# Eight experts, two layers: x in two loads of four experts, finer last pieces of w2, stores moved between queues

## Chip, cores and metric

One Trainium2 chip, one core. The metric is device time in microseconds; the time of a kernel is the median of its runs. Engines are named as in the profile: PE (matmul), PEld (weight load of PE), DVE (VectorE), ACT (ScalarE), POOL (GpSimd), SP (SyncE).

## The reference

```python
n_experts, capacity, hidden, expert_hidden = 8, 256, 512, 2048
h = np.matmul(x, w1)        # (8,256,512) @ (8,512,2048)
h = np.maximum(h, 0)
return np.matmul(h, w2).astype(np.float32)   # (8,256,2048) @ (8,2048,512)
```

All inputs and the output are float32. Each expert has 4.19 MB of w1, 4.19 MB of w2, 0.52 MB of x and 0.52 MB of output.

## The kernel before

The kernel works in bf16 on PE. Weights are cast on the way in: `load_w1` (L55) and `load_w2` (L59) issue DMAs from POOL that read f32 and write bf16. One load is 128 rows of 32 KB in memory, one for each partition; w2 of the last expert comes in four pieces of 6, 5, 3 and 2 row groups (a row group is 128 rows of w2, one for each partition). The tag "w1" and the tag "w2" have four buffers each, so a load of expert e waits until expert e - 4 has been used. POOL issues its DMAs in program order: it stands still at the first that has to wait.

x comes in f32 from SP, one load of 512 KB for each expert with rows of 4 KB (`load_x`, L51), four experts ahead. `transpose_x` (L65) casts it on ACT (L67), transposes it on PE in eight 128x128 blocks into one PSUM bank (L71) and copies it out on DVE (L75).

`first_layer` (L77) makes the hidden layer in eight groups of 8 matmuls (L83), each 128x128 weights by 256 columns of x; the relus alternate between ACT (L93) and DVE (L91). `second_layer` (L98) makes 32 matmuls of 512 columns (L107), 16 row groups of w2 times two halves of the rows; DVE copies out one half (L115), ACT the other (L116), and SP stores the expert (L121), or SP and ACT half of it each for the last expert (L118, L119).

The order is written out by hand (`manual_schedule`, L49; L124 to L145): first and second layer of experts 0 to 4 in turn, then the three first layers of experts 5, 6 and 7, then their three second layers. All weight loads are put on POOL ahead of the computation in this same order. The transposes of expert e + 1 stand behind the first layer of expert e on PE. On SP, the load of x of expert e + 4 stands behind the store of expert e. In the text below, w1(3) is w1 of expert 3, and so on.

Of the kernel before, what the change touches and what calls it, by code (L numbers as in the profile page):

```python
# [1 line left out]

# [5 lines left out]


@with_exitstack  # L10
def kernel(
    ctx: ExitStack,
    tc: tile.TileContext,
    x: bass.AP,
    w1: bass.AP,
    w2: bass.AP,
    out: bass.AP,
):
    nc = tc.nc
    P = 128  # L20
    bf = mybir.dt.bfloat16
    f32 = mybir.dt.float32

    E, C, H = x.shape
    F = w1.shape[2]
    MT = C // P
    KT1 = H // P
    KT2 = F // P
    AHEAD = 4


    x_r = x.rearrange("e (p mt) k -> e p mt k", p=P)
    w1_r = w1.rearrange("e (p kt) n -> e p kt n", p=P)
    w2_r = w2.rearrange("e (p kt) n -> e p kt n", p=P)
    out_r = out.rearrange("e (p mt) n -> e p mt n", p=P)

    const = ctx.enter_context(tc.tile_pool(name="const", bufs=1))
    wpool = ctx.enter_context(tc.tile_pool(name="weights", bufs=4))
    xpool = ctx.enter_context(tc.tile_pool(name="xs", bufs=AHEAD))
    tpool = ctx.enter_context(tc.tile_pool(name="xts", bufs=2))  # L40
    hpool = ctx.enter_context(tc.tile_pool(name="hidden", bufs=4))
    opool = ctx.enter_context(tc.tile_pool(name="outs", bufs=3))
    ps_h = ctx.enter_context(tc.tile_pool(name="ps_h", bufs=4, space=bass.MemoryType.PSUM))
    ps_o = ctx.enter_context(tc.tile_pool(name="ps_o", bufs=4, space=bass.MemoryType.PSUM))

    x_sb, w1_sb, w2_sb, xt, ht = {}, {}, {}, {}, {}


    ctx.enter_context(tc.manual_schedule())  # L49

    def load_x(e):  # L51
        x_sb[e] = xpool.tile([P, MT, H], f32, tag="x", name="x_sb")
        nc.sync.dma_start(x_sb[e][:], x_r[e])

    def load_w1(e):  # L55
        w1_sb[e] = wpool.tile([P, KT1, F], bf, tag="w1", name="w1_sb")
        nc.gpsimd.dma_start(w1_sb[e][:], w1_r[e])  # L57

    def load_w2(e):  # L59
        w2_sb[e] = wpool.tile([P, KT2, H], bf, tag="w2", name="w2_sb")  # L60
        cuts = (0, KT2) if e < E - 1 else (0, 6, 11, 14, 16)
        for lo, hi in zip(cuts, cuts[1:]):
            nc.gpsimd.dma_start(w2_sb[e][:, lo:hi, :], w2_r[e, :, lo:hi, :])  # L63

    def transpose_x(e):  # L65
        x_bf = tpool.tile([P, MT, H], bf, tag="xb", name="x_bf")
        nc.scalar.copy(x_bf[:], x_sb[e][:])  # L67
        pt = ps_o.tile([P, KT1, MT, P], bf, tag="ps_o", name="pt_tr")
        for kt in range(KT1):
            for mt in range(MT):  # L70
                nc.tensor.transpose(  # L71
                    pt[:, kt, mt, :], x_bf[:, mt, kt::KT1], identity[:]
                )
        xt[e] = tpool.tile([P, KT1, C], bf, tag="xt", name="xt_sb")
        nc.vector.tensor_copy(xt[e][:], pt[:].rearrange("p k m q -> p k (m q)"))  # L75

    def first_layer(e):  # L77
        ht[e] = hpool.tile([P, KT2, C], bf, tag="ht", name="ht_sb")
        for g in range(KT2 // 2):
            ph = ps_h.tile([P, 2, C], f32, tag="ps_h", name="pt_h")  # L80
            for i in range(2):
                for kt in range(KT1):
                    nc.tensor.matmul(  # L83
                        ph[:, i, :],
                        w1_sb[e][:, kt, 2 * g + i::KT2],
                        xt[e][:, kt, :],
                        start=(kt == 0),
                        stop=(kt == KT1 - 1),
                    )
            if g % 2:  # L90
                nc.vector.tensor_relu(ht[e][:, 2 * g:2 * g + 2, :], ph[:])  # L91
            else:
                nc.scalar.activation(  # L93
                    ht[e][:, 2 * g:2 * g + 2, :], ph[:],
                    mybir.ActivationFunctionType.Relu,
                )

    def second_layer(e):  # L98
        last = e == E - 1
        po = [  # L100
            ps_o.tile([P, H], f32, tag="ps_o", name=f"pt_o{mt}") for mt in range(MT)
        ]
        order = [(kt, mt) for kt in range(KT2) for mt in range(MT)]
        if last:
            order = order[:-4] + [(kt, mt) for mt in range(MT) for kt in (KT2 - 2, KT2 - 1)]
        for kt, mt in order:
            nc.tensor.matmul(  # L107
                po[mt][:],
                ht[e][:, kt, mt * P:(mt + 1) * P],
                w2_sb[e][:, kt, :],  # L110
                start=(kt == 0),
                stop=(kt == KT2 - 1),
            )
        o = opool.tile([P, MT, H], f32, tag="o", name="out_sb")
        nc.vector.tensor_copy(o[:, 0, :], po[0][:])  # L115
        nc.scalar.copy(o[:, 1, :], po[1][:])  # L116
        if last:
            nc.sync.dma_start(out_r[e, :, 0, :], o[:, 0, :])  # L118
            nc.scalar.dma_start(out_r[e, :, 1, :], o[:, 1, :])  # L119
        else:  # L120
            nc.sync.dma_start(out_r[e], o[:])  # L121


    order = []  # L124
    for e in range(E - 3):
        order += [(1, e), (2, e)]
    order += [(1, e) for e in range(E - 3, E)] + [(2, e) for e in range(E - 3, E)]

    for e in range(AHEAD):
        load_x(e)  # L130
    for layer, e in order:
        (load_w1 if layer == 1 else load_w2)(e)
        if (layer, e) == (1, 0):
            identity = const.tile([P, P], bf, name="identity")
            make_identity(nc, identity)
    transpose_x(0)
    for layer, e in order:
        if layer == 1:
            first_layer(e)
            if e + 1 < E:  # L140
                transpose_x(e + 1)
        else:
            second_layer(e)
            if e + AHEAD < E:
                load_x(e + AHEAD)  # L145


# [1 line left out]
_INS = ['x', 'w1', 'w2']  # L149
_OUTS = [((8, 256, 512), 'float32')]  # L150


# [23 lines left out]
```

## Time and profile before

| | |
|---|---|
| median of 11 runs | 186.9 us (186.77 to 188.67) |
| profiled execution | 188.32 us |
| its span, first to last instruction | 186.5 us |
| mean granted PE clock | 0.927 |
| PE busy | 132.9 us (71%) |
| PE weight loads busy | 91.3 us (49%) |
| DVE, ACT, POOL busy | 33.2, 32.6, 10.9 us |
| DMA | 5192 packets, 42.06 MB at the destination |

The span leaves out what lies around the first and last instruction; the profiled execution's own time is 1.8 us longer. In the profile, a timeline line gives start, length, engine, line of the code, operation, output and inputs, count, and in brackets how long the engine had been idle and what ended it. A stretch gives each engine's busy time in a window with the granted clock, the mean busy share of the 16 DMA engines and what they moved. Packet records can overlap, so a DMA share can pass 1. "q0" holds the DMAs that POOL issues, "q1" those of SP, "q10" those of ACT.

### The profile page before, as it was taken

The numbers are of one execution on the slowest core, as the hardware profiler recorded it, in microseconds if no ns is written. First come the engines' busy times: TensorE is split into PE (matmuls) and PEld (weight loads), VectorE is DVE, ScalarE is ACT, GpSimd is POOL, SyncE is SP. The second block draws the span as 40 slices with busy tenths as digits, with TensorE's granted clock in tenths as the row PEclk, the third lists the DMA queues.
The fourth block names the chain that finished last, engine by engine and source line by source line (L and its number), as shares of the span: only waits on it lengthen the run. The fifth ranks groups of instructions, "written<-read, shape, count | busy, mean of one in ns | idle before, by whom it ended". The sixth has DMA issues, their size and how long they took to land.

```text
span 186.5 us, 1894 instructions
## 1 busy us (share of the span) xinstructions
PE 132.9 (71%) x832; PEld 91.3 (49%) x832; DVE 33.2 (18%) x48; ACT 32.6 (18%) x49; POOL 10.9 (6%) x25
## 2 busy tenths in 40 slices
PE   0204959488595988749894795929969695949990
PEld 0103944187232873238741693407969693414440
DVE  0100240113101141101311032011224241010101
ACT  3100330124001240102401123011242421010101
POOL 7300010101000010000201101001000000000000
PEclk9999999999879699966999799995899999988999
DMA  6989999999999999999989899999999999999913
GB/s 222 270 211 249 243 214 225 221 237 240 217 275 212 258 230 220 259 213 264 239 205 281 203 259 235 213 275 211 242 240 225 225 218 197 204 216 263 217 58 114
DMA packets 5192, 42.06 MB, mean 225 GB/s; under 512 B 576, under 2 KB 576, under 8 KB 3264
## 3 DMA queue, kind: packets, MB, share of 16 engines
q0 software_dynamic: 2736, 33.56, 84.6%
q1 hardware_dynamic: 2304, 8.13, 11.6%
q10 hardware_dynamic: 144, 0.26, 0.4%
q8 instruction: 6, 0.10, 0.2%
q14 instruction: 2, 0.02, 0.0%
HBM read 71.30 MB, written 4.19 MB: 405 GB/s over the span
## 4 chain that ended last, share of the span: by engine, by line
PE 55%; DMA 24%; another core or an unknown queue 10%; ACT 3%; issue 2%; POOL 1%; DVE 1%; ACTq 0%; POOLq 0%
PE pt_o L107 28%; PE pt_h L83 26%; DMA w_sb<-in_w_dram 24%; ACT x_bf L67 3%; PE pt_tr L71 2%; DVE xt_sb L75 1%; POOL w_sb L57 1%; DVE out_sb L115 0%; POOL w_sb L63 0%; POOL identity masks.py:199 0%; POOL identity masks.py:197 0%; ACT ht_sb L93 0%; ACTq L116 0%; POOLq masks.py:199 0%
## 5 line engine op out<-in xcount | busy, mean ns | idle before, releaser
L83 PE MATMUL pt_h<-xt_sb,w_sb 128*128 128x256 bf16 x512 | 67.9, 302 | 28.6 <-DMA w_sb<-in_w_dram 27.0
L83 PEld LDWEIGHTS <-w_sb 128*128 128x128 bf16 x512 | 61.8, 149 | 35.9 <-DMA w_sb<-in_w_dram 30.0
L107 PE MATMUL pt_o<-w_sb,ht_sb 128*128 128x512 bf16 x256 | 59.7, 394 | 9.9 <-DMA w_sb<-in_w_dram 9.9
L107 PEld LDWEIGHTS <-ht_sb 128*128 128x128 bf16 x256 | 25.7, 101 | 42.1 <-issue 15.4
L91 DVE TENSOR_SCALAR ht_sb<-pt_h 128x512 bf16<-128x512 f32 x32 | 22.1, 692 | 75.3 <-PE pt_h L83 75.3
L93 ACT ACTIVATE ht_sb<-pt_h 128x512 bf16<-128x512 f32 x32 | 19.1, 597 | 74.8 <-PE pt_h L83 74.8
L116 ACT COPY out_sb<-pt_o 128x512 f32<-128x512 f32 x8 | 4.7, 585 | 72.2 <-PE pt_o L107 72.2
L115 DVE COPY out_sb<-pt_o 128x512 f32<-128x512 f32 x8 | 5.5, 691 | 62.9 <-PE pt_o L107 62.9
L71 PE MATMUL pt_tr<-identity,x_bf 128*128 128x128 bf16 x64 | 5.5, 234 | 10.4 <-ACT x_bf L67 10.4
L71 PEld LDWEIGHTS <-x_bf 128*128 128x128 bf16 x64 | 4.1, 119 | 12.1 <-ACT x_bf L67 12.1
L57 POOL DMA_DIRECT2D w_sb<-in_w_dram x8 | 4.4, 556 | 75.6 <-PE pt_h L83 74.8
L67 ACT CAST x_bf<-x_sb 128x1024 bf16<-128x1024 f32 x8 | 8.3, 1037 | 2.1 <-DMA x_sb<-in_x_dram 2.1
L63 POOL DMA_DIRECT2D w_sb<-in_w_dram x11 | 6.0, 543 | 39.9 <-DMA w_sb<-in_w_dram 24.1
L75 DVE COPY xt_sb<-pt_tr 128x1024 bf16<-128x1024 bf16 x8 | 5.5, 692 | 11.1 <-PE pt_tr L71 11.1
L67 ACT ACT_TABLE_LOAD x1 | 1.3, 1283 | 0.7 <-PEq L160 0.7
masks.py:199 POOL TENSOR_SCALAR_AFFINE_SELECT identity<-identity 128x128 bf16<-128x128 bf16 x1 | 0.3, 287 | 0.1
masks.py:197 POOL MEMSET identity<- 128x128 bf16 x1 | 0.2, 223 | 0.0
L160 POOL MEMSET const-float32-0.0<- 128x1 f32 x1 | 0.1, 98 | 0.2 <-issue 0.2
L160 POOL MEMSET const-bfloat16-1.0<- 128x1 bf16 x1 | 0.1, 101 | 0.0
L160 POOL MEMSET const-uint8-127<- 128x1 uint8 x1 | 0.1, 101 | 0.0
L160 POOL MEMSET const-float32-1.0<- 128x1 f32 x1 | 0.1, 98 | 0.0
## 6 DMA issues: line engine op xcount, KB each, us to landing
w_sb<-in_w_dram POOLq DMA_DIRECT2D x15, 2048.0 KB, 66.3
x_sb<-in_x_dram SPq DMA_DIRECT2D x8, 512.0 KB, 25.6
out_dram<-out_sb SPq DMA_DIRECT2D x7, 512.0 KB, 15.4
w_sb<-in_w_dram POOLq DMA_DIRECT2D x1, 768.0 KB, 70.1
w_sb<-in_w_dram POOLq DMA_DIRECT2D x1, 640.0 KB, 70.1
w_sb<-in_w_dram POOLq DMA_DIRECT2D x1, 384.0 KB, 60.5
w_sb<-in_w_dram POOLq DMA_DIRECT2D x1, 256.0 KB, 51.2
out_dram<-out_sb ACTq DMA_DIRECT2D x1, 256.0 KB, 2.7
```

Source lines behind the costliest of these rows:

```text
L57: nc.gpsimd.dma_start(w1_sb[e][:], w1_r[e])
L63: nc.gpsimd.dma_start(w2_sb[e][:, lo:hi, :], w2_r[e, :, lo:hi, :])
L67: nc.scalar.copy(x_bf[:], x_sb[e][:])
L71: nc.tensor.transpose(pt[:, kt, mt, :], x_bf[:, mt, kt::KT1], identity[:])
L75: nc.vector.tensor_copy(xt[e][:], pt[:].rearrange("p k m q -> p k (m q)"))
L83: nc.tensor.matmul(ph[:, i, :], w1_sb[e][:, kt, 2 * g + i::KT2], xt[e][:, kt, :], start=(kt == 0), stop=(kt == KT1 - 1),)
L91: nc.vector.tensor_relu(ht[e][:, 2 * g:2 * g + 2, :], ph[:])
L93: nc.scalar.activation(ht[e][:, 2 * g:2 * g + 2, :], ph[:], mybir.ActivationFunctionType.Relu,)
L107: nc.tensor.matmul(po[mt][:], ht[e][:, kt, mt * P:(mt + 1) * P], w2_sb[e][:, kt, :], start=(kt == 0), stop=(kt == KT2 - 1),)
L115: nc.vector.tensor_copy(o[:, 0, :], po[0][:])
L116: nc.scalar.copy(o[:, 1, :], po[1][:])
L160: nc = _bacc.Bacc("TRN2", target_bir_lowering=False, num_devices=1)
```

## The change

- x is loaded in two loads of four experts each (G = 2), with rows of 16 KB in memory: the first as f32 from SP and cast on ACT in four instructions, the second cast to bf16 by the DMA itself, from POOL, between w1(1) and w2(1). Partition p then holds 8 rows in sequence, so one expert lies in 32 partitions, and all four experts of a load are transposed together: 32 blocks, in four rounds of 8 with two strided copies each, one on DVE and one on ACT. The first four experts are transposed at the start, the other four within the first layer of expert 2, one round after every second group.
- The weight tags have three buffers instead of four, the hidden layer three instead of four, the outputs five instead of three.
- w2(6) comes in three pieces of 6, 5 and 5 row groups, w2(7) in seven of 4, 4, 3, 2, 1, 1 and 1.
- Stores of experts 0 to 4 are issued by POOL, at places written out between the weight loads: those of 0 and 1 behind w2(3) and w2(4), that of 2 behind w2(5), those of 3 and 4 behind w2(6).
- Stores of experts 5 and 6 stay on SP and get a wait for the third last piece of w2(7). The last expert's halves follow on SP and ACT as before.
- The last second layer runs its matmuls in plain order of row groups.

```diff
-    AHEAD = 4
+    G = 2
+    EG = E // G
+    J = EG * C // P
+    J2 = J // MT
+    WB = 3
...
-    wpool = ctx.enter_context(tc.tile_pool(name="weights", bufs=4))
+    wpool = ctx.enter_context(tc.tile_pool(name="weights", bufs=WB))
+    hpool = ctx.enter_context(tc.tile_pool(name="hidden", bufs=3))
+    opool = ctx.enter_context(tc.tile_pool(name="outs", bufs=5))
...
+    x_f = const.tile([P, J, H], f32, name="x_f")
+    x_b = [const.tile([P, J, H], bf, name=f"x_b{g}") for g in range(G)]
+    xt = [const.tile([P, KT1, EG, C], bf, name=f"xt{g}") for g in range(G)]
...
-        cuts = (0, KT2) if e < E - 1 else (0, 6, 11, 14, 16)
+        cuts = {E - 2: (0, 6, 11, 16), E - 1: (0, 4, 8, 11, 13, 14, 15, 16)}.get(e, (0, KT2))
...
+    def transpose_x(g, kts):
+        for kt in kts:
+            pt = ps_o.tile([P, J, P], bf, tag="ps_o", name="pt_tr")
+            for j in range(J):
+                nc.tensor.transpose(pt[:, j, :], x_b[g][:, j, kt::KT1], identity[:])
+            src = pt[:].rearrange("p (j m) (e l) -> p m e l j", m=MT, e=EG)
             for mt in range(MT):
+                dst = xt[g][:, kt, :, mt * P:(mt + 1) * P].rearrange(
+                    "p e (l j) -> p e l j", j=J2
                 )
+                if mt % 2:
+                    nc.scalar.copy(dst, src[:, mt])
+                else:
+                    nc.vector.tensor_copy(dst, src[:, mt])
+    def first_layer(e, between=()):
...
+            if g % 2 and between:
+                between.pop(0)()
...
+    def store(e):
+        nc.gpsimd.dma_start(out_r[e], o_sb[e][:])
+    nc.sync.dma_start(x_f[:], x_r[0])
+    load_w1(0)
+    make_identity(nc, identity)
+    load_w2(0)
+    load_w1(1)
+    nc.gpsimd.dma_start(x_b[1][:], x_r[1])
+    load_w2(1)
+    load_w1(2)
+    load_w2(2)
+    for j in range(0, J, 2):
+        nc.scalar.copy(x_b[0][:, j:j + 2, :], x_f[:, j:j + 2, :])
+    transpose_x(0, range(KT1))
+    first_layer(0)
+    load_w1(3)
+    second_layer(0)
+    load_w2(3)
+    store(0)
+    first_layer(1)
+    load_w1(4)
+    second_layer(1)
+    load_w2(4)
+    store(1)
+    first_layer(2, [lambda kt=kt: transpose_x(1, [kt]) for kt in range(KT1)])
+    load_w1(5)
+    second_layer(2)
+    first_layer(3)
+    load_w1(6)
+    second_layer(3)
+    first_layer(4)
+    load_w1(7)
+    load_w2(5)
+    store(2)
+    load_w2(6)
+    store(3)
+    second_layer(4)
+    store(4)
+    load_w2(7)
+    for e in (5, 6, 7):
+        first_layer(e)
+    for e in (5, 6, 7):
+        second_layer(e)
+    for e in (5, 6):
+        d = nc.sync.dma_start(out_r[e], o_sb[e][:])
+        tc.add_manual_dep(
+            d.ins,
+            pieces[-3].ins.name,
...
+    nc.sync.dma_start(out_r[7, :, 0, :], o_sb[7][:, 0, :])
+    nc.scalar.dma_start(out_r[7, :, 1, :], o_sb[7][:, 1, :])
```

## The prediction

> **What bounds the kernel now.** I read the page's slices and queue table first, then the matrix engine's timeline, then the end of the run in stretches.
>
> ```profile
> DMA  6989999999999999999989899999999999999913
> q0 software_dynamic: 2736, 33.56, 84.6%
> q1 hardware_dynamic: 2304, 8.13, 11.6%
> HBM read 71.30 MB, written 4.19 MB: 405 GB/s over the span
> ```
>
> The 16 DMA engines are busy from start to end, 97% over all queues; only the last two slices are not full. So the span is a stream of bytes and a tail. PE is busy 71% and waits for weights in nearly every layer:
>
> ```profile
> 37.99 7.21 PE L83 MATMUL pt_h<-xt_sb,w_sb 128*128 128x256 bf16 x64 [3.38 <-DMA w_sb<-in_w_dram]
> 59.87 8.87 PE L83 MATMUL pt_h<-xt_sb,w_sb 128*128 128x256 bf16 x64 [2.25 <-DMA w_sb<-in_w_dram]
> 81.87 9.96 PE L83 MATMUL pt_h<-xt_sb,w_sb 128*128 128x256 bf16 x64 [3.92 <-DMA w_sb<-in_w_dram]
> 125.89 10.13 PE L83 MATMUL pt_h<-xt_sb,w_sb 128*128 128x256 bf16 x64 [3.47 <-DMA w_sb<-in_w_dram]
> 156.55 7.07 PE L107 MATMUL pt_o<-w_sb,ht_sb 128*128 128x512 bf16 x32 [1.90 <-DMA w_sb<-in_w_dram]
> 166.25 15.57 PE L107 MATMUL pt_o<-w_sb,ht_sb 128*128 128x512 bf16 x64 [2.64 <-DMA w_sb<-in_w_dram]
> ```
>
> A start after "<-DMA" is the landing of a load. The last line is the key: the second layers of experts 6 and 7 run 15.57 us without a gap, so after w2 of expert 6 landed at 166.2 the matrix engine, not the DMA, set the end. When did the weights end? In stretches (columns: PE, PEld, DVE, ACT, POOL busy, clock, DMA share, GB/s):
>
> ```profile
> 175.75:176.00 0.25, 0.25 (x3) 0.10 (x1) 0.00 (x0) 0.00 (x0) 0.00 (x0) 1.00 0.60 115
> 176.75:177.00 0.25, 0.25 (x3) 0.13 (x2) 0.00 (x0) 0.00 (x0) 0.00 (x0) 1.00 0.97 344
> 177.00:177.25 0.25, 0.25 (x3) 0.11 (x2) 0.00 (x0) 0.00 (x0) 0.00 (x0) 1.00 1.02 410
> 178.25:178.50 0.25, 0.25 (x3) 0.13 (x2) 0.00 (x0) 0.00 (x0) 0.00 (x0) 1.00 0.00 0
> ```
>
> A casting load counts its bf16 bytes, so weights show as 200 to 220 GB/s; 344 to 410 is the store of expert 6, issued at 175.6. From 176.25 to 178.25 about 0.57 MB moved, which is that store's 0.52. The weights' data thus ends at **E = 176.4**, and PE works until 181.84: 5 us of matmuls are exposed behind the last byte.
>
> **What the skill says.** (1) "DMA: Bandwidth & Descriptors", Issuing engines are not separate DMA queues: all issuers share the 16 DMA engines. The trace agrees: 84.6 + 11.6% fills them, so moving stores from SP to POOL makes no bandwidth. (2) The same page, Queues, rings and completion order: each DMA engine takes its rings in turn. Agrees in kind: the 0.5 MB stores beside weights take 15.4 us (median) to land, 2.7 us at the end with no weights. (3) The same page, Anatomy of one DMA: about 2.0 us fixed for each DMA from POOL. The trace shows it overlapped where loads are queued: from 125.9 to 156.5 three loads land, with most of one store, 10.2 us each. (4) "TensorE: Matmul & The Clock Gate", What's actually happening: half clock after some 3.4 us idle, until as much busy time has passed. The trace has it after shorter gaps too: after the 2.64 us gap at 166.25, 128x512 matmuls start 0.43 us apart and later 0.22.
>
> ```profile
> 166.63 0.15 PEld L107 LDWEIGHTS <-ht_sb 128*128 128x128 bf16 x1 [0.28 <-issue]
> 167.06 0.15 PEld L107 LDWEIGHTS <-ht_sb 128*128 128x128 bf16 x1 [0.28 <-issue]
> ```
>
> **Prices out of the trace.** One 4.19 MB weight load: 156.5 to 166.2 (almost undisturbed) 9.7 us, 432 GB/s. Two loads with one x and one store: 37.9 to 59.8, 59.8 to 81.8, 81.8 to 103.8, 22.0 each; less 19.4, an x plus a store cost 2.6. From 16.4 to 37.9, two loads and about two x: 21.5, so an x is 1.05. Left for a store is 1.5.
>
> **Part by part, the stream (what moves E).**
> - Store of expert 5 leaves the stream (SP now waits for the third last piece): -1.3 (the row above, minus the little that moved before 165.7). The store of expert 6 already flowed after E: 0.
> - x: eight loads, 8 x 1.05 = 8.4, go. The first half as f32 from SP stays at 4 x 1.05 = 4.2, since it still interleaves with w1 of expert 0; the second, cast on POOL, has weight-like rows: 2.1 MB at 432 GB/s = 4.85. Sum +0.65; bounds -0.3 (wide rows make the f32 half cheaper, 3.3) and +1.3 (both at 4.85).
> - Stores 0 to 4 now lie in POOL's own queue, in line with the weights instead of interleaved. No row shows that. Bounds for one: 1.2 (0.52 MB at 432 GB/s) and 3.2 (with the skill's 2.0 us not overlapped). Nearest row: the last store alone, 0.52 MB from 183.4 to 184.8, 1.4 us. I take 1.4: 5 x (1.4 - 1.5) = -0.5; bounds -1.5 and +8.5.
> - Five more DMAs for w2, three of them one row group (2 KB rows): +0.3 estimate; from 0 (the four pieces of before show no loss) to 0.8.
> Sum: -1.3 + 0.65 - 0.5 + 0.3 = -0.85; E' = **175.55**.
>
> **Does the stream stay fed?** Weight buffers fall from four to three, and POOL runs in order. In before, POOL waits at 104.10, 115.60 and 126.12 for a landing, each the load eight DMAs earlier: eight may be in flight. I walked POOL's 30 DMAs with 9.7 us a load. Start: x of four experts lands with w1(0), about 16.4 + 2 x 1.05 = 18.5; then four casts of 1.04 (ACT, 4.2), the last 24 transposes at a cold 0.13 (3.1) and copies of 0.6 to 0.7: first matmul near 26.7 instead of 16.5. This 10 us is covered: the loads up to w2(2) need no release and last to 71, w1(3) is issued at about 36. PE needs some 17 us per expert and the stream 19.4, so PE has caught up when w2(1) lands, about 52. Later slack (issue to the moment when the queue would be empty): w1(6) 33 us, w1(7) 21. Pieces b to g of w2(7) wait for the landing eight DMAs back, the last at about 164, 10 us early. Stores on POOL wait for copies done long before. So 0. If the cover failed, each us late there is a us.
> The 32 transposes of the second half, inside the first layer of expert 2 (64 to 73), cost PE 32 x 0.08 = 2.6 us, and eight copies of some 0.65 on DVE and ACT delay relus behind them: w2(2) lands at 71, so the second layer starts 2 us late, and next w1(3) lands at 81: 0. The casts and transposes ahead of experts 6 and 7 (idle 0.75 + 0.78 twice) go: 0 too, since PE waited 1.90 for w2(5) after.
>
> **The tail.** w2(6) comes in three pieces, so its layer starts before all of it is there: w2(5) lands near 152.5, its layer ends by 161, w2(6) is done by 168, and w2(7)'s first piece lands at 168.8. A half-clock spell there costs 8 x 0.21 = 1.7 us and is made up while the pieces come (9.7 us of DMA for 7.07 of PE). After E': landing 0.5 (as the last store: data to 184.8, landed 185.3), two matmuls 0.9 (half clock taken; 0.45 at full), then as before from last matmul to the end 186.5 - 181.84 = 4.66. That is E' + 6.1. Ahead of the last half store on SP stand the stores of 5 and 6: issued at about E' - 0.7, data from E' + 0.2, 2 x 1.36 = 2.7, done at E' + 2.9; the halves' data would start at E' + 2.95 (1.55 after the last matmul, as 183.4 - 181.84). They just fit; +0.1, from 0 to 1.4 if they start later. End: 175.55 + 6.2 = **181.75**, 4.75 less than 186.5. With the 188.32 - 186.5 = 1.82 around the span: 183.57.
>
> **Beside the median.** Runs of before fall in two groups, near 186.85 and 188.5; the profiled 188.32 is of the upper. The distance, 1.65, is what the 8 half-clock matmuls at 166.25 cost on the exposed chain (8 x 0.21), so I hold the usual run to end near 184.9. In after that spell is hidden, and the forecast is the same for both groups: **183.6** against 186.9, -1.8%.
>
> **Rivals.**
> A, the forecast: 183.6, chance 0.60.
> B, the tail is dearer: the stores of 5 and 6 delay the last halves by a full 1.4, or PE is behind when the last piece lands: 185.0, 0.15. For it: SP's queue is in order, and its wait sits ahead of the last half store. Against: the 2.7 us fit by my count.
> C, cheaper transfers: wide x rows 0.9 less, stores in line at 1.2 (-1.0), +0.2 of the small pieces not seen: 181.7, 0.12.
> D, slower: stores in line break the weights' stream. A store's writes wait behind weight packets no longer, but the weights behind it now wait for it, and with the 2.0 us receipt not overlapped one costs up to 3.2: 183.6 + 5 x 1.8 = 192.6. It decides from (187.8 - 183.6)/5 + 1.4 = 2.25 us a store. Against it: queued loads show no such gap. 0.13, with most of it near 188.
> Range: A's own bounds are 182 to 186; with half of C and the lower edge of D, 181.9 to 186.8. About 0.5% is what a measurement can tell from no change. Faster by more: A, C and nearly all of B, 0.79; same: the rest between, 0.09; slower: most of D, 0.12.
>
> **What would show it.** Right: PE waits between the pieces of w2(7), and the last matmul ends within 2 us of the last weight byte, near 177; first matmul of a layer at 23 to 28; no empty DMA slice before 175. For D: DMA share clearly under 0.9 at the stores in POOL's queue and w1(5) landing later than 123. For B: over 5.2 us from last matmul to end. Wrong altogether: POOL's w1(6) or w1(7) issued after the stream ran dry, or a PE chain with no gap to the end.

## The result, and the profile after

The changed kernel takes 183.62 us (median of 12 runs, 183.29 to 184.26) against 186.85 us of before (47 runs, 186.68 to 189.0). The ratio of the means is 0.9804, with a 95% interval of 0.9777 to 0.983; the medians alone give 0.983, because before's mean (187.32) also holds its upper group of times. Forecast was 183.6. The profiled execution took 183.59 us with a span of 181.5, against a forecast span of 181.75.

First the page of the changed kernel: the slices of the DMA, the two big queues (packets, MB, share of 16 engines' span) and the bytes.

```profile
DMA  6999999999999999999999999999999999999996
q0 software_dynamic: 4320, 37.23, 94.2%
q1 hardware_dynamic: 576, 3.41, 5.0%
HBM read 71.30 MB, written 4.19 MB: 416 GB/s over the span
```

The same bytes in 5 us less. In before, the DMA row ended "9913": it had two thin slices. Now it is full up to the last one. A stretch with little DMA at the end is gone. In before that stretch was filled by matmuls; the timeline of PE from the landing of w2(5) on shows where they are now:

```profile
153.26 13.97 PE L117 MATMUL pt_o<-w_sb,ht_sb 128*128 128x512 bf16 x64 [2.64 <-DMA w_sb<-in_w_dram]
169.08 1.90 PE L117 MATMUL pt_o<-w_sb,ht_sb 128*128 128x512 bf16 x8 [1.85 <-DMA w_sb<-in_w_dram]
171.52 5.68 PE L117 MATMUL pt_o<-w_sb,ht_sb 128*128 128x512 bf16 x24 [0.54 <-DMA w_sb<-in_w_dram]
```

Experts 5 and 6 are done by 167.2 (64 matmuls), expert 7 waits for its pieces at 169.08 and 171.52, and the rest keeps the pace of the landings. In before, the 64 matmuls of experts 6 and 7 began only at 166.25. The chain that ended last now closes with the DMA (start, length, what):

```profile
165.81 10.76 DMA w_sb<-in_w_dram
...
176.61 0.61 PE pt_o L117 x2
...
177.24 0.59 ACT out_sb L126
```

Two matmuls stand behind the last landing. The last matmul ends at 177.21; in before it was 181.84. The end of the run in stretches (busy PE, PEld, DVE, ACT, POOL; clock; DMA share; GB/s):

```profile
174.50:175.00 0.50, 0.50 (x4) 0.25 (x3) 0.00 (x0) 0.00 (x0) 0.00 (x0) 1.00 0.85 137
175.00:175.50 0.50, 0.50 (x4) 0.20 (x2) 0.00 (x0) 0.00 (x0) 0.00 (x0) 1.00 0.48 78
175.50:176.00 0.50, 0.50 (x4) 0.23 (x3) 0.00 (x0) 0.00 (x0) 0.00 (x0) 1.00 0.32 51
176.00:176.50 0.50, 0.50 (x3) 0.16 (x2) 0.00 (x0) 0.00 (x0) 0.00 (x0) 1.00 0.79 303
177.50:178.00 0.50, 0.00 (x0) 0.00 (x0) 0.21 (x1) 0.32 (x1) 0.00 (x0) 1.00 0.96 393
180.00:180.50 0.50, 0.00 (x0) 0.00 (x0) 0.00 (x0) 0.00 (x0) 0.00 (x0) 0.50 0.30 111
```

The weights thin out from 174.7 to 176.0. From 176.0 to 180.2 the held stores and the last two halves (1.57 MB) flow at some 375 GB/s in the mean, close to the 381 to 389 that the last store alone had in before.

### The profile page after: what moved, and what is told of

Its sections match the earlier page's. It is cut to its first block, busy times and chain, and to the rows that moved or that the text cites. A ratio compares the mean times of both kernels' runs of the same rounds, so it can differ in the third digit from the quotient of the medians.

```text
span 181.5 us, 1885 instructions
## 1 busy us (share of the span) xinstructions
PE 128.0 (71%) x832; PEld 89.2 (49%) x832; DVE 32.8 (18%) x48; ACT 33.3 (18%) x53; POOL 16.7 (9%) x36
## 4 chain that ended last, share of the span: by engine, by line
DMA 60%; PE 27%; another core or an unknown queue 6%; POOL 3%; issue 1%; ACT 0%; POOLq 0%
DMA w_sb<-in_w_dram 60%; PE pt_o L117 13%; PE pt_h L97 13%; POOL w_sb L71 1%; PE pt_tr L80 1%; POOL w_sb L62 1%; ACT out_sb L126 0%; POOL out_dram L129 0%; POOL x_b L137 0%; POOL identity masks.py:199 0%; POOL identity masks.py:197 0%; POOLq masks.py:199 0%; POOLq L215 0%; POOLq L204 0%
## 5 line engine op out<-in xcount | busy, mean ns | idle before, releaser
L97 PE MATMUL pt_h<-xt,w_sb 128*128 128x256 bf16 x512 | 64.2, 289 | 16.1 <-DMA w_sb<-in_w_dram 15.5
L117 PE MATMUL pt_o<-w_sb,ht_sb 128*128 128x512 bf16 x256 | 58.7, 387 | 17.0 <-DMA w_sb<-in_w_dram 17.0
L97 PEld LDWEIGHTS <-w_sb 128*128 128x128 bf16 x512 | 59.1, 147 | 21.8 <-DMA w_sb<-in_w_dram 18.4
L80 PE MATMUL pt_tr<-identity,x_b 128*128 128x128 bf16 x64 | 6.6, 264 | 16.1 <-ACT x_b L142 16.1
L80 PEld LDWEIGHTS <-x_b 128*128 128x128 bf16 x64 | 5.4, 127 | 16.9 <-ACT x_b L142 16.9
L71 POOL DMA_DIRECT2D w_sb<-in_w_dram x16 | 8.6, 541 | 49.8 <-DMA w_sb<-in_w_dram 26.3
L62 POOL DMA_DIRECT2D w_sb<-in_w_dram x8 | 4.4, 552 | 81.0 <-PE pt_h L97 80.2
L89 DVE COPY xt<-pt_tr 128x512 bf16<-128x512 bf16 x8 | 5.5, 686 | 18.3 <-PE pt_tr L80 18.3
L142 ACT CAST x_b<-x_f 128x1024 bf16<-128x1024 f32 x4 | 3.9, 1041 | 11.4 <-DMA x_f<-in_x_dram 11.4
L87 ACT COPY xt<-pt_tr 128x512 bf16<-128x512 bf16 x8 | 4.7, 585 | 7.0 <-DVE xt L89 7.0
L129 POOL DMA_DIRECT2D out_dram<-out_sb x5 | 2.7, 539 | 18.5 <-DMA w_sb<-in_w_dram 18.2
```

The lines of the kernel that those rows point to most:

```text
L80: nc.tensor.transpose(pt[:, j, :], x_b[g][:, j, kt::KT1], identity[:])
L87: nc.scalar.copy(dst, src[:, mt])
L89: nc.vector.tensor_copy(dst, src[:, mt])
L97: nc.tensor.matmul(ph[:, i, :], w1_sb[e][:, kt, 2 * g + i::KT2], xt[e // EG][:, kt, e % EG, :], start=(kt == 0), stop=(kt == KT1 - 1),)
L117: nc.tensor.matmul(po[mt][:], ht[e][:, kt, mt * P:(mt + 1) * P], w2_sb[e][:, kt, :], start=(kt == 0), stop=(kt == KT2 - 1),)
L142: nc.scalar.copy(x_b[0][:, j:j + 2, :], x_f[:, j:j + 2, :])
```

## The experiments

A single edit was made to the changed kernel unless the text says otherwise. Beside every group of experiments before was run again, and the median of its lower group was 186.7 to 186.8 each time, so medians can be set beside the 183.62. The ratio, by contrast, takes in both groups of before and moves with how many of its runs fell in the upper one. The changed kernel's own runs spread over 1.0 us; a difference under some 0.4 says nothing.

| edit | median us (range) | ratio to before, 95% interval |
|---|---|---|
| before with the pieces | 185.76 (185.69 to 185.92) | 0.9915, 0.9881 to 0.9949 |
| before with the pieces and the hold | 184.34 (184.10 to 184.81) | 0.9843, 0.9808 to 0.9877 |
| w2(6) whole | 185.45 (183.71 to 186.63) | 0.9882, 0.9844 to 0.992 |
| no hold | 185.87 (185.27 to 187.79) | 0.9936, 0.9914 to 0.9958 |
| stores 0 to 4 on SP | 184.35 (183.98 to 185.98) | 0.9841, 0.9786 to 0.9897 |
| stores 2 to 4 ahead of w2(5) | 186.20 (185.34 to 188.11) | 0.9939, 0.9913 to 0.9965 |
| stores 0 to 4 on SP, 2 to 4 held | 183.41 (183.20 to 183.63) | 0.977, 0.9726 to 0.9815 |
| x as before | 183.81 (183.47 to 184.01) | 0.9783, 0.9743 to 0.9823 |
| hold two pieces less | 183.58 (183.07 to 184.64) | 0.9783, 0.9734 to 0.9831 |
| that, and the last copies in halves | 183.65 (183.13 to 184.54) | 0.9791, 0.9747 to 0.9835 |
| w2(7) in four pieces | 184.72 (183.72 to 186.21) | 0.985, 0.98 to 0.99 |
| before, unchanged | 187.68 (186.68 to 188.75) | 0.9994, 0.9954 to 1.0034 |

**Only the pieces, on the kernel before.**

```diff
-        cuts = (0, KT2) if e < E - 1 else (0, 6, 11, 14, 16)
+        cuts = {E - 2: (0, 6, 11, 16), E - 1: (0, 4, 8, 11, 13, 14, 15, 16)}.get(e, (0, KT2))
...
-        if last:
-            order = order[:-4] + [(kt, mt) for mt in range(MT) for kt in (KT2 - 2, KT2 - 1)]
```

> The kernel before with only w2(6) in three and w2(7) in seven pieces (and the last layer's matmuls in plain row-group order). Theory: PE is off the end, but the store of expert 6 now comes about 7 us earlier and lies in the stream of w2(7), so the weights end at 176.4 + 1.3 + 0.3 = 178.0; with 0.9 to landing, 0.6 of matmuls and 4.5 behind them the span is 184.0 and the time 185.8, about 1.1 below the 186.85 of before. Rival (pieces are the whole gain): 183.6. Rival (x and the queue of the stores are the gain, pieces nothing): 186.9.

185.76, as expected to 0.1. The matmuls are off the end, but the store of expert 6 has moved into the weights' stream. From 174.5 to 176.5 this run's DMA moves 303 to 336 GB/s, where weights alone show some 200 (207 from 173 to 174), and the last piece lands at 178.93 instead of 176.57. Two of these stretches:

```profile
175.00:175.50 0.50, 0.50 (x4) 0.20 (x2) 0.00 (x0) 0.00 (x0) 0.00 (x0) 1.00 1.07 336
175.50:176.00 0.50, 0.42 (x2) 0.10 (x1) 0.00 (x0) 0.00 (x0) 0.00 (x0) 1.00 1.08 332
```

With the matmuls done earlier, the store comes earlier too, and takes its time from the weights: the pieces alone give 1.1 us.

**The pieces and the hold, on the kernel before.** The same, and:

```diff
-            nc.sync.dma_start(out_r[e], o[:])
+            d = nc.sync.dma_start(out_r[e], o[:])
+            if e >= E - 3:
+                tc.add_manual_dep(d.ins, pieces[-3].ins.name, ...)
```

> The kernel before with the pieces and with the stores of experts 5 and 6 held for the third last piece, x and the other stores as before. Theory (pieces and hold together are the whole gain; x and the stores on POOL cancel): weights end at 176.4 - 1.3 + 0.3 = 175.4, span 181.6, time 183.5 to 183.9, equal to the changed kernel within 0.4. Rival (wide rows of x and stores in POOL's queue bring a part): 184.3 or more.

184.34: 2.5 us of the 3.2 come from these two edits of the end. But 0.7 is missing, and this is where the theory was incomplete. The timeline of PE (of the slowest of the six runs, 184.81) has one line from w2(5) on:

```profile
157.07 20.88 PE L107 MATMUL pt_o<-w_sb,ht_sb 128*128 128x512 bf16 x94 [0.82 <-DMA w_sb<-in_w_dram]
```

w2(5) lands 3.8 us later than in the changed kernel, and three second layers without a gap (two matmul records are missing) last to 177.95. The stream alone doesn't set the end here: the matmuls do again, at full clock, 0.74 later than the last matmul of the changed kernel.

**w2(6) whole.**

```diff
-        cuts = {E - 2: (0, 6, 11, 16), E - 1: (0, 4, 8, 11, 13, 14, 15, 16)}.get(e, (0, KT2))
+        cuts = {E - 1: (0, 4, 8, 11, 13, 14, 15, 16)}.get(e, (0, KT2))
```

> The changed kernel with w2 of expert 6 in one load again. Theory (the gain is mostly the matmul chain that no longer hangs on the landing of all of w2(6)): w2(6) lands near 164.9, then 64 matmuls run without a gap for 14.0 us (15.6 with a half-clock spell), the last ends at 178.9 to 180.6 instead of 177.2, so the time rises by 1.7 to 3.4 us, to 185.3 to 187.0. Rival (the gain is in cheaper x and store transfers): the time stays near 183.6.

The median, 185.45, is inside what was expected, but the runs lie in three groups: 183.7 to 183.9 (three runs of twelve), 185.2 to 185.8, and 186.4 to 186.6. The profiled execution, 183.72, is of the fastest, which lies where the rival had it, though not for the rival's reason:

```profile
153.15 7.07 PE L117 MATMUL pt_o<-w_sb,ht_sb 128*128 128x512 bf16 x31 [2.93 <-DMA w_sb<-in_w_dram]
163.70 13.97 PE L117 MATMUL pt_o<-w_sb,ht_sb 128*128 128x512 bf16 x63 [3.49 <-DMA w_sb<-in_w_dram]
```

w2(6) lands at 163.70, 1.2 earlier than expected. PE waits 3.49 for all of it and then has 14 us without a gap, which at full clock ends only 0.46 later than in the changed kernel (last matmul 177.67). In before the same landing came at 166.25: the stores of experts 3 and 4 are no longer ahead of it, and w2(6) comes 2.55 earlier here. So, by this profile, the place of the stores takes this chain off the end too, as long as the clock is full. A half-clock spell of 1.6 to 1.9 us, such as other profiles show after such a wait, would fall on the end, and the second group is some 1.7 higher; the third isn't explained. The higher groups have no profile, so this is not shown.

**No hold.** The `tc.add_manual_dep` of stores 5 and 6 is taken out.

> The changed kernel with the stores of experts 5 and 6 on SP as soon as they are ready. Theory (the hold takes 2.6 us of stores out of the weights' stream and puts them into the tail where most of the time is idle): the weights end 2.6 later, the tail is about 0.3 shorter, time about 185.7, 2.1 above the changed kernel. Rival B of the prediction (the held stores delay the last halves by 1.4): the tail gets that back, so time 184.5 or less.

185.87 where 185.7 was expected: two stores of the stream's time come back. PE shows the stretched landings of w2(7):

```profile
170.63 1.90 PE L117 MATMUL pt_o<-w_sb,ht_sb 128*128 128x512 bf16 x8 [3.24 <-DMA w_sb<-in_w_dram]
173.95 1.89 PE L117 MATMUL pt_o<-w_sb,ht_sb 128*128 128x512 bf16 x8 [1.42 <-DMA w_sb<-in_w_dram]
```

The matmuls of the first two pieces start 1.6 and 2.4 us later than 169.08 and 171.52. The rival, that the held stores are in the way of the last halves, fell.

**Stores 0 to 4 on SP.**

```diff
     def store(e):
-        nc.gpsimd.dma_start(out_r[e], o_sb[e][:])
+        nc.sync.dma_start(out_r[e], o_sb[e][:])
```

> The changed kernel with the stores of experts 0 to 4 issued by SP when ready instead of by POOL in line with the weights. Theory (a store in line costs 1.27 us of the stream, one interleaved from SP 1.5): 5 x 0.23 = 1.1 us slower, 184.7. Rival (all issuers share the same DMA engines, a store costs the same either way): 183.6.

184.35 in the median: slower by 0.7, but not for the reason expected. (Four runs are at 184.0 to 184.4 and two at 185.8 and 186.0; the profile is of the four.) On SP's timeline the held stores go out at the landing of the third last piece, so their start marks how far the weights are:

```profile
175.01 0.81 SPq L179 DMA_DIRECT2D out_dram<-out_sb  x2
```

In the changed kernel it is 175.33: the stream is no later with the stores on SP. What is later is w2(5):

```profile
157.13 20.88 PE L117 MATMUL pt_o<-w_sb,ht_sb 128*128 128x512 bf16 x94 [3.11 <-DMA w_sb<-in_w_dram]
```

The stores of experts 2, 3 and 4 are now sent when ready, the last of them at 124.0:

```profile
37.96 86.40 SPq L129 DMA_DIRECT2D out_dram<-out_sb  x5
```

Each lands within 15.5 us, so their bytes pass ahead of w2(5) instead of behind it, and the three last layers end at 178.0 as in the run with the pieces and the hold. From this a new theory: the place of these stores counts, not their queue. Two runs told these apart.

**Stores 2 to 4 ahead of w2(5), still on POOL.**

```diff
-    load_w2(5)
     store(2)
-    load_w2(6)
     store(3)
     second_layer(4)
     store(4)
+    load_w2(5)
+    load_w2(6)
     load_w2(7)
```

> The changed kernel with the stores of experts 2, 3 and 4 still on POOL, but ahead of w2(5) instead of behind w2(5) and w2(6). Theory formed on the stores-on-SP run (what the queue of the stores is worth is their place: behind w2(5) they let it land 3 x 1.27 = 3.8 us earlier, and the three last second layers, 20.9 us of matmuls at full clock, stay off the end): w2(5) lands near 157.1, matmuls run without a gap to 178.0 or later, time 184.3 or a little more. Rival (POOL in line is cheaper than SP interleaved, wherever it stands): 183.6.

186.20, 2.6 us slower, so the place alone loses it, and 1.9 more than expected:

```profile
157.22 22.83 PE L117 MATMUL pt_o<-w_sb,ht_sb 128*128 128x512 bf16 x96 [5.09 <-DMA w_sb<-in_w_dram]
```

w2(5) lands at 157.22 as worked out. But PE has idled 5.09 us before it and starts at half clock: 22.83 for the chain instead of 20.88, and the 1.95 more fall on the end (180.05).

**Stores 0 to 4 on SP, held.** Those of 2, 3 and 4 come back behind w2(5) and w2(6), this time from SP.

```diff
-        nc.gpsimd.dma_start(out_r[e], o_sb[e][:])
+        nc.sync.dma_start(out_r[e], o_sb[e][:])
...
+    for e, k in ((2, 5), (3, 8), (4, 8)):
+        d = nc.sync.dma_start(out_r[e], o_sb[e][:])
+        tc.add_manual_dep(d.ins, pieces[k].ins.name, ...)
```

> The changed kernel with the stores of experts 0 to 4 on SP, those of 2, 3 and 4 held there for the landing of w2(5) (store 2) and of w2(6) (stores 3 and 4). Theory (place, not queue): w2(5) lands near 153.3 again, gaps between the pieces of w2(7), 183.6. Rival (the queue): 184.3 as with the stores on SP unheld.

183.41, the same as the changed kernel within its spread. w2(5) is early and the gaps between the pieces are back:

```profile
152.81 15.70 PE L117 MATMUL pt_o<-w_sb,ht_sb 128*128 128x512 bf16 x72 [2.59 <-DMA w_sb<-in_w_dram]
169.40 1.89 PE L117 MATMUL pt_o<-w_sb,ht_sb 128*128 128x512 bf16 x8 [0.90 <-DMA w_sb<-in_w_dram]
```

So behind w2(5) the queue is worth nothing that can be measured. Ahead of it the two queues differ, 184.35 from SP against 186.20 from POOL: in POOL's queue the three stores stand together right in front of w2(5), which comes 13.97 after w1(7) (143.25 to 157.22), and PE waits 5.09; from SP they are spread over earlier loads, w2(5) comes 10.32 after w1(7), and PE waits 3.11 and keeps the full clock.

**x as before.** Eight f32 loads with rows of 4 KB on SP, and the cast on ACT and the transposes expert by expert; `load_x` and `transpose_x` are those of the kernel before.

```diff
-    nc.sync.dma_start(x_f[:], x_r[0])
+    for e in range(4):
+        load_x(e)
...
-    nc.gpsimd.dma_start(x_b[1][:], x_r[1])
...
     second_layer(0)
+    load_x(4)
```

> The changed kernel with x as in the kernel before: eight f32 loads from SP with 4 KB rows, cast on ACT and transposed expert by expert; the rest as changed. Theory by the ledger of the prediction (eight narrow loads 8.4 us against 4.2 + 4.85): 0.65 us faster, 183.0. Rival (wide rows are cheaper for the stream): 184.3 or more. Rival (x costs its bytes however it comes): 183.6.

183.81: neither the 0.65 faster of the prediction's sum nor the slower of the first rival; the second rival, 183.6, fits. The rewriting of x, the largest part of the diff, gives or costs nothing that can be told. The same run shows that a slow start of the last layers is hidden:

```profile
153.40 15.66 PE L114 MATMUL pt_o<-w_sb,ht_sb 128*128 128x512 bf16 x62 [2.51 <-DMA w_sb<-in_w_dram]
169.35 1.90 PE L114 MATMUL pt_o<-w_sb,ht_sb 128*128 128x512 bf16 x8 [0.29 <-DMA w_sb<-in_w_dram]
```

Experts 5 and 6 took 15.66 here, 13.97 in the profile of the changed kernel, and PE still had to wait for the first piece.

**The hold two pieces less** (`pieces[-5]` for `pieces[-3]`).

> The changed kernel with the stores of experts 5 and 6 held for the fifth last piece of w2(7) (row groups 8 to 11) instead of the third last. Theory (in the changed kernel the DMA engines are half idle from 175.0 to 176.0, since the held stores are issued only at 175.3 and 175.8; two pieces earlier, 1.8 us, they fill that hole and clear the way of the last halves): up to 0.6 us faster, 183.0 to 183.3. Rival (stores that start before the last pieces slow these by as much as they fill): 183.6 to 184.5.

183.58: nothing is gained. The hole is filled, as these stretches show, and a new one opens in front of the last halves, which wait for their copies. The last matmuls end at 177.21, as in the changed kernel, so the stores haven't slowed the last pieces either:

```profile
175.00:175.50 0.50, 0.50 (x4) 0.20 (x2) 0.00 (x0) 0.00 (x0) 0.00 (x0) 1.00 1.07 352
175.50:176.00 0.50, 0.50 (x4) 0.26 (x3) 0.00 (x0) 0.00 (x0) 0.00 (x0) 1.00 1.09 393
178.00:178.50 0.50, 0.00 (x0) 0.00 (x0) 0.00 (x0) 0.00 (x0) 0.00 (x0) 1.00 0.16 66
...
171.49 5.72 PE L117 MATMUL pt_o<-w_sb,ht_sb 128*128 128x512 bf16 x24 [0.56 <-DMA w_sb<-in_w_dram]
```

**That, and the last expert's copies and stores in halves of 256 columns.**

```diff
-    nc.sync.dma_start(out_r[7, :, 0, :], o_sb[7][:, 0, :])
-    nc.scalar.dma_start(out_r[7, :, 1, :], o_sb[7][:, 1, :])
+    for lo, hi in ((0, H // 2), (H // 2, H)):
+        nc.sync.dma_start(out_r[7, :, 0, lo:hi], o_sb[7][:, 0, lo:hi])
+        nc.scalar.dma_start(out_r[7, :, 1, lo:hi], o_sb[7][:, 1, lo:hi])
```

> The changed kernel with the stores of experts 5 and 6 held two pieces less, and the last expert's copies and stores in halves of 256 columns, so that the first half's store starts while the second is copied. Theory (behind the last matmul stand a copy of 0.6 to 0.7, 0.8 to first data, 1.4 of transfer; half of a copy is saved, two more issues and narrower rows are paid): 0.3 faster than the changed kernel, 183.3. Rival (the transfer starts at the same time because issue and rows cost what the copy saves): 183.6.

183.65: nothing either. The first issue on SP moved from 177.74 to 177.50 only, and each queue issues twice. None of these versions beats the changed kernel by more than its spread.

**w2(7) in four pieces.**

```diff
-... E - 1: (0, 4, 8, 11, 13, 14, 15, 16)}
+... E - 1: (0, 6, 11, 14, 16)}
...
-            pieces[-3].ins.name,
+            pieces[-2].ins.name,
```

> The changed kernel with w2 of expert 7 in four pieces of 6, 5, 3 and 2 row groups, the held stores still waiting for the piece behind which two row groups follow. Theory (a finer end leaves fewer matmuls behind the last landing): four matmuls instead of two behind it, 0.4 to 0.5 us more, and three DMAs less in the stream, 0 to 0.3 us back: 183.7 to 184.1. Rival (the number of the pieces matters for the start of the layer too): 184.5 or more.

184.72, with half the runs at 183.7 to 184.2 and half at 185.3 to 186.2. The profiled one, 186.21, shows why:

```profile
171.13 8.77 PE L117 MATMUL pt_o<-w_sb,ht_sb 128*128 128x512 bf16 x32 [4.22 <-DMA w_sb<-in_w_dram]
171.93 0.15 PEld L117 LDWEIGHTS <-ht_sb 128*128 128x128 bf16 x1 [0.26 <-issue]
172.36 0.15 PEld L117 LDWEIGHTS <-ht_sb 128*128 128x128 bf16 x1 [0.28 <-issue]
```

The first piece is larger, so it lands 2 us later; PE has idled 4.22 us, starts at half clock (0.43 us a matmul) and doesn't catch up. So small pieces at the front of the last load matter as well as at its end: they shorten the wait ahead of the half clock. This profile is of the slowest run; the three runs near 184 fit the 183.7 to 184.1 of the theory, but that they lack the spell isn't shown.

**Before again**, for a profile of its lower group.

> The kernel before, unchanged, for a second profile. Theory of the prediction (the two groups of its times differ by a half-clock spell in the exposed chain at 166): if this profile falls in the lower group (span near 185.0), its last 64 matmuls take about 14.0 us instead of 15.57. Rival (the groups differ in the stream): the chain takes 15.6 and starts 1.6 earlier.

The profiled execution fell in the upper group (188.75), with the same slow chain, so the question stays open:

```profile
166.62 15.66 PE L107 MATMUL pt_o<-w_sb,ht_sb 128*128 128x512 bf16 x64 [2.64 <-DMA w_sb<-in_w_dram]
```

That the lower group lacks the spell isn't shown. The spans of all runs speak for it (184.8 to 185.7 and 186.4 to 187.0, where 184.9 was forecast for the lower), and so do the chains of 13.97 in other kernels: 15.57 and 15.66 are 1.6 to 1.7 longer, and the groups lie 1.6 apart.

## Why the prediction was right, by its steps

- **What bounded the kernel before**: right. 64 matmuls hung on the landing of all of w2(6). Given w2(6) whole, the changed kernel loses 1.8 in the median, though next to nothing in its three fastest runs (183.7 to 183.9), where w2(6) lands at 163.70 instead of 166.25.
- **Stores 5 and 6 out of the stream, 1.3 for that of 5**: right in kind and size. Without the hold, 2.25 us come back for two stores. The prediction saw only one in the old stream; the pieces alone would have drawn in the second, which the pieces-only run shows.
- **Stores 0 to 4 in line, -0.5 in the stream**: the price was about right, the gain was not there. Between these two landings in the changed kernel two loads and the store of expert 1 pass. They take 20.61, two loads alone 19.4, so this store cost 1.2:

```profile
103.42 8.88 PE L97 MATMUL pt_h<-xt,w_sb 128*128 128x256 bf16 x64 [3.91 <-DMA w_sb<-in_w_dram]
124.03 8.87 PE L97 MATMUL pt_h<-xt,w_sb 128*128 128x256 bf16 x64 [3.86 <-DMA w_sb<-in_w_dram]
```

  That of expert 0 cost 1.9 (two loads from 82.08 to 103.42, 21.34), and the three ahead of w2(5) 1.4 each (13.97 less 9.7). These lie around the 1.4 taken. What failed is the other side of the difference: interleaved from SP, where 1.5 was taken, they lengthen the stream no more than in line (third last piece at 175.01 against 175.33). The gain of the edit is 0.7 and goes another way: behind w2(5), stores 2 to 4 let it land at 153.26 instead of 157.1. The prediction had nearly this landing in its walk (152.5) and didn't see it as a gain; with it late, the chain of 20.88 us sets the end again.
- **x, +0.65**: not there. The second half cost what was worked out (38.52 to 53.02 is 14.5, less 9.7 leaves 4.8 for 4.85), but with x as before the time is the same within the spread. The 1.05 for a narrow x, got by dividing intervals, was too fine a reading. So the two terms +0.65 and -0.5 were each about nothing, and their errors cancelled by luck.
- **Five more DMAs, +0.3**: not told apart.
- **The start**: first matmul of a layer forecast at 26.7 and, as a sign of being right, at 23 to 28; found at 20.09. That sign failed. x was to land together with w1(0) at 18.5. It landed at 13.4: of 3.4 MB that the DMA had moved by then (254 GB/s), 2.1 MB were x and 1.3 MB weights in bf16, which is 2.6 MB of f32 read. So x had nearly as much of the DMA as the weights and, being half of w1(0)'s size, was done first. That the late start costs nothing was right. With x as before the first matmul starts at 16.43 and the time is the same, and here PE has caught up by 53.02, where it waits 7.28 for w2(1):

```profile
13.39 3.88 ACT L142 CAST x_b<-x_f 128x1024 bf16<-128x1024 f32 x4 [11.38 <-DMA x_f<-in_x_dram]
20.09 1.12 PE L97 MATMUL pt_h<-xt,w_sb 128*128 128x256 bf16 x3
53.02 8.89 PE L117 MATMUL pt_o<-w_sb,ht_sb 128*128 128x512 bf16 x32 [7.28 <-DMA w_sb<-in_w_dram]
```

- **Three buffers cost nothing**: right by the trace: w1(7) is issued at 112.60, and the DMA row has no thin slice after the first. No kernel with other counts was run.
- **The tail**: the last landing came at 176.57 (forecast 176.05), as the weights thin out over more than 1 us. From the last matmul to the end it was 4.29 (forecast 4.76). The held stores fit, as worked out; moved earlier they give nothing.
- **The sum**: that 183.59 came out where 183.57 was worked out is partly luck. The last matmul ended 0.26 late (177.21 for 176.95), the tail was 0.47 shorter, and the time around the span, taken as 1.82 from before, was 2.09 (2.0 to 2.25 in the twelve runs). Why this last part grew isn't known. None of these is over 0.5, so they don't touch the mechanism.
- **The median**: one group of times was forecast, since half-clock spells are hidden. The runs lie within 1.0 us, where before has two groups 1.6 apart, and those with the lowest and the highest mean clock (0.905 and 0.958) took 183.29 and 183.43. The x-as-before profile shows such a spell absorbed.
- **A reading of the stores**: the 2.7 us to land without weights beside it is that of a half store; the whole one of expert 6 took 3.1. Nothing rests on it.

Of the rivals, the dearer tail, the cheaper transfers and the broken stream were all refuted by the time; the last also by the 1.2 to 1.9 for a store in line.

## What to carry to other kernels

When a kernel is bound by a stream of loads, look also at what work hangs on the last large landing: cutting the last loads so that the matmuls keep up with them, and keeping stores out of their way, was worth the whole gain here, and the rewritten input path nothing that could be measured. A store took about the same time out of the stream from either queue here; what counted is which load it stood in front of. After an edit that frees one resource, ask which transfers now come earlier and into what they run: the pieces without the hold gave a third of the gain.

## What the runs showed of the hardware

- The last bytes of the stream thin out. Over 174.7 to 176.0 the DMA share falls to 0.3, and the last piece lands only at 176.57. Other work can fill that hole without delaying the landing (352 to 393 GB/s there with the hold two pieces less, last matmul at the same 177.2).
- The half clock depends on more than the length of a wait. After waits of 2.64 us the same 64 matmuls took 15.57 (before, at 166.25) and 13.97 (changed, at 153.26). A wait of 2.51 (x as before) had it; waits of 3.11 (stores on SP) and 3.49 (w2(6) whole) did not; after 4.22 and 5.09 us the profiles at hand show it. The Trainium skill ("TensorE: Matmul & The Clock Gate", What's actually happening) calls the activity window free-running, which fits that equal waits end differently. Its figure of some 3.4 us idle does not fit the waits of 2.51 and 2.64; the measurement decides.
- Reads and writes over the span of 181.5 us come to 416 GB/s. A queued casting load with no store beside it takes 9.7 us (124.03 to 133.73 in the changed kernel), 432 GB/s of source bytes.
